# Two-layer hybrid decoder trunk: gate and up products with the stream stationary and the weights moving, the activations transposed afterwards

## The chip, the cores and the metric

The kernel runs on one core of one Trainium2 chip. Its time is the device time of one launch in microseconds; of three runs before the change the median is 1235.31 us (1235.24 to 1237.77). A profile of one execution stands beside it, whose span, from the first to the last instruction, is 1231.7 us. Engines are named as in the profile: PE is TensorE's matmul row and PEld its row of weight loads, DVE is VectorE, ACT is ScalarE, POOL is GpSimd, and SP issues most of the transfers.

## The reference

256 tokens of 1024 features pass through two layers. Each layer is a half-step feed-forward network, a mixing block (three branches, gated and projected), and a second half-step feed-forward network; a last RMSNorm ends it. Everything is float32.

```python
D_MODEL = 1024; SEQ = 256; DEPTH = 2; D_FF = 2816

def swiglu(x, w_gate, w_up, w_down):
    return (jax.nn.silu(x @ w_gate) * (x @ w_up)) @ w_down

for l in range(DEPTH):
    h = h + 0.5 * swiglu(rmsnorm(h, ffn1_norm[l]), ffn1_w_gate[l], ffn1_w_up[l], ffn1_w_down[l])
    u = rmsnorm(h, mix_norm[l])
    ...                                        # latent attention, differential attention, pooling
    h = h + merged @ w_out[l]
    h = h + 0.5 * swiglu(rmsnorm(h, ffn2_norm[l]), ffn2_w_gate[l], ffn2_w_up[l], ffn2_w_down[l])
return rmsnorm(h, final_norm)
```

The change touches `x @ w_gate` and `x @ w_up` of the four feed-forward networks: 1024 features in, 2816 out, for 256 tokens.

## The kernel before, in words

Every large product is made of three matmuls (`mm3`, lines 162 to 165). Each operand is held as a high part of 12 bits and a low part, both float32r; the product is high by high, low by high and high by low, added up in one PSUM bank. The stream's parts (`uhi`, `ulo`, eight tiles of 128 features by 256 tokens) come from `Norm`; they carry the norm's gain, but not yet each token's factor `r`. A weight tile is 1 MB: one transfer on SP's queue (line 150), then `wsplit` makes the parts in two pieces of 1024 columns each, the high one by a cast on ACT (line 158) and the low one by a subtraction on DVE (line 159). There are three buffers each for the raw tile, the high and the low part, so a cast may start when the matmuls are done with the tile three before it.

In a matmul one operand is stationary (128 by 128, loaded by a weight load) and the other moves through. The two kinds of product in this kernel are:

- Weights stationary: out comes transposed (features on the partitions, 256 tokens along the free dimension), and each matmul moves 256 columns, the tokens. The gate and up products are of this kind, and so are a few in the mixing block.
- Stream stationary (`gemm_tokens`, line 167): the tokens are on the partitions, 128 at a time, and each matmul moves 512 columns of weights. The down products, the gates and most of the mixing block are of this kind.

A feed-forward network (`ffn`, line 265) goes over the 2816 columns in eleven chunks of 256. A chunk takes one tile of gate weights and one of up weights, 48 matmuls for each (2 output tiles of 128 columns, 8 feature tiles, 3 products). In the first chunk of a network the halves of the stream are done one after the other, since its second half is only just being made. The token factors are needed along the free dimension here; `Norm.row` (line 238) spreads them with one small matmul (line 244). The products are multiplied by the factors on DVE (lines 302 and 304), the gate goes through Silu on ACT (line 307), DVE multiplies gate and up (line 309), and `split_evac` splits the result into `ghi` (ACT, line 258) and `glo` (DVE, line 259). These are already in the layout that the down product wants as its stationary operand.

The program is written in order, and a scheduler of the language places the instructions in each engine's queue before the launch; on the chip each queue then runs strictly in its order, with semaphores between the engines. PSUM has four banks for products (`acc`), three for transposes and scores (`tr`) and one for attention outputs.

Of the kernel before, what the change touches and what calls it, by code (L numbers as in the profile page):

```python
# [44 lines left out]
def plan():  # L45
    """Weight tiles in the order of their use: (array, layer, first row tile, row tiles, first column, columns)."""
# [5 lines left out]
    def ffn(layer, pre):  # L52
        for c in range(0, DFF, S):
            for w in ("gate", "up"):
                add(f"{pre}_w_{w}", layer, 0, KD, c, S)
        for half in range(2):
            for k in range(0, KF, 4):
                add(f"{pre}_w_down", layer, k, min(4, KF - k), half * 512, 512)
# [27 lines left out]
def trunk(ctx, tc, x, xt, positions, wall, small, lamrow, fnorm, out):  # L86
# [51 lines left out]
    # the input's loads, which go between those of the first weights  # L138
# [28 lines left out]
    def gemm_tokens(specs, xh, xl, n, before=None, tail=1):  # L167
        """Products with tokens on the partitions: one bank for each half of the tokens.

        The first half of the tokens is done ahead of the second in the last tiles, tail of them."""  # L170
# [3 lines left out]
        for part in parts:  # L174
            w = [(s[2] + j, hi[:, j, :], lo[:, j, :]) for s in part for hi, lo in (wsplit(s),) for j in range(s[3])]
            if before and part is parts[-1]:
                before()
            order = [(k, wh, wl, t) for k, wh, wl in w for t in range(2)]
# [7 lines left out]
    def rsqrt_mean(dst, src, n):  # L186
        """dst = (src / n + eps) ** -0.5"""
# [3 lines left out]
    class Norm:  # L191
        """The transposed, scaled stream in two parts, and each token's factor, half by half."""
# [26 lines left out]
        def first(self, k):  # L219
            """A tile of the same from the input, which comes in both layouts."""  # L220
# [17 lines left out]
        def row(self):  # L238
            """The factors along the free dimension, on every partition."""
# [15 lines left out]
    def split_evac(hi, lo, src, scale=None):  # L255
        """PSUM or SBUF -> the two parts, times a constant or a column."""
# [8 lines left out]
    def ffn(l, pre, u, following, midway=None):  # L265
        ghi = [big([P, 8, S], F32R, "ghi") for _ in range(3)]
        glo = [big2([P, 8, S], F32R, "glo") for _ in range(3)]
        for c in range(0, DFF, S):
            if c == 1024 and midway:
                midway(g[:, 0, :2])  # L270
            # transposed products, weights stationary: two tiles of each
            opened = bool(opening)
            w = [wsplit((f"{pre}_w_{n}", l, 0, KD, c, S)) for n in ("gate", "up")]
            if c == 0:
                # a bank for each tile, so that the first half of the stream serves them all
                ps = [[b()[:, :S] for _ in range(2)] for b in (acc, trp)]
                halves = [range(0, 4), range(4, 8)]
                order = [(n, i, k) for ks in halves for n in range(2) for i in range(2) for k in ks]
                if opened:
                    order = [(n, i, k) for n in range(2) for k in range(KD) for i in range(2)]  # L280
            else:
                banks = [acc() for _ in range(2)]
                ps = [[b[:, i * S:(i + 1) * S] for i in range(2)] for b in banks]
                order = [(n, i, k) for n in range(2) for i in range(2) for k in range(KD)]
# [4 lines left out]
            if c == 0:  # L289
# [4 lines left out]
                rb = u.row()  # L294
            g = tp.tile([P, 2, S], F32, tag="A", name="g", bufs=4)
            sg = tp.tile([P, 2, S], F32, tag="B", name="sg")
# [553 lines left out]
```

## Time and profile before

| | |
|---|---|
| median of three runs | 1235.31 us |
| span of the profiled execution | 1231.7 us |
| median less that span | 3.6 us |
| PE busy | 1216.1 us, 99% of the span |
| PEld busy | 1108.6 us, 90% |
| DVE busy | 792.4 us, 64% |
| ACT busy | 576.9 us, 47% |
| mean granted clock of TensorE | 0.999 |
| read from memory | 210.85 MB, 172 GB/s over the span |

The profile gives no launch time of its own for that execution; what lies around its span is taken as the difference to the median. Busy time is the union of an engine's instructions. Matmuls overlap in their pipeline: the mean duration of one is longer than the distance between the starts of two, so the cost of a stream of them is read from the starts in the timeline, not from the mean durations. In a timeline row the columns are start, duration, engine, line, operation, tiles and shapes, and the count of merged instructions.

### The profile page before, as it was taken

Reading aid. Unit: us, or ns where it says so; the run is one execution under the profiler, and the core shown is the slowest. Engines: PE = TensorE matmul, PEld = TensorE weight load, DVE = VectorE, ACT = ScalarE, POOL = GpSimd, SP = SyncE. Lnnn points to the kernel's source line nnn. Section 1 sums busy time; section 2 is a strip of 40 time slices with the busy share of each in tenths; the row PEclk is TensorE's granted clock in tenths of the full one; section 3 lists DMA queues with packets and bytes.
Section 4 is the critical chain, followed back from the end, with each engine's and each line's share of the span. In section 5 each row is a group of like instructions: output and inputs, shape, how many; then the busy total and the mean of one; then the engine's idle time right before and its main releaser. Section 6 shows DMA issues by size and latency. Waiting matters only on the chain.

```text
span 1231.7 us, 19142 instructions
## 1 busy us (share of the span) xinstructions
PE 1216.1 (99%) x7912; PEld 1108.6 (90%) x7912; DVE 792.4 (64%) x1281; ACT 576.9 (47%) x891; POOL 69.3 (6%) x126
## 2 busy tenths in 40 slices
PE   7999999999999999999999999999999999999997
PEld 7999989998788899998899998899978888999986
DVE  6776655777757666664576664568686485766653
ACT  5454444446544554443454443455455444544442
POOL 0000000700100000000000000024010000000000
PEclk9999999999999999999999999999999999999999
DMA  8655455325345545554555555544343554455551
GB/s 276 239 184 181 175 181 191 120 93 189 137 171 176 192 172 179 181 191 168 187 199 176 191 182 188 175 146 145 110 165 135 177 202 171 171 188 188 189 171 68
DMA packets 34631, 213.13 MB, mean 173 GB/s; under 512 B 4080, under 2 KB 5488, under 8 KB 10992
## 3 DMA queue, kind: packets, MB, share of 16 engines
q1 hardware_dynamic: 33408, 210.52, 48.3%
q10 hardware_dynamic: 1136, 1.40, 0.4%
q8 instruction: 62, 1.02, 0.3%
q14 instruction: 25, 0.20, 0.1%
HBM read 210.85 MB, written 1.05 MB: 172 GB/s over the span
## 4 chain that ended last, share of the span: by engine, by line
PE 94%; DVE 3%; issue 2%; ACT 0%; DMA 0%; SPq 0%; POOLq 0%; POOL 0%
PE acc L163 28%; PE acc L164 28%; PE acc L165 28%; PE o L589 2%; PE tr L555 2%; PE tr L582 1%; PE tr L546 1%; PE tr L206 1%; DVE lo L159 1%; PE tr L163 1%; PE tr L165 1%; PE tr L164 1%; DMA xT<-xt 0%; PE tr L602 0%; PE acc L658 0%
## 5 line engine op out<-in xcount | busy, mean ns | idle before, releaser
L158 ACT CAST hi<-raw 128x1024 fp32r<-128x1024 f32 (+2 forms) x416 | 403.6, 1005 | 512.4 <-issue 326.3
L159 DVE TENSOR_TENSOR lo<-raw,hi 128x1024 fp32r<-128x1024 f32 (+2 forms) x416 | 481.4, 1173 | 223.1 <-ACT hi L158 222.2
L163 PE MATMUL acc<-uhi,hi 128*128 128x256 f32 x1536 | 439.2, 286 | 5.6 <-ACT hi L158 5.6
L165 PE MATMUL acc<-uhi,lo 128*128 128x256 f32 x1536 | 437.7, 285 | 1.5 <-DVE lo L159 1.5
L164 PE MATMUL acc<-ulo,hi 128*128 128x256 f32 x1536 | 437.7, 285 | 0.0
L163 PEld LDWEIGHTS acc<-uhi,hi 128*128 128x128 f32 x1536 | 296.7, 193 | 5.8 <-ACT hi L158 5.6
L165 PEld LDWEIGHTS acc<-uhi,lo 128*128 128x128 f32 x1536 | 296.6, 193 | 2.3 <-DVE lo L159 2.1
L164 PEld LDWEIGHTS acc<-ulo,hi 128*128 128x128 f32 x1536 | 296.8, 193 | 0.3
L164 PE MATMUL acc<-lo,ghi 128*128 128x512 f32 x352 | 137.4, 390 | 0.0
L165 PE MATMUL acc<-hi,glo 128*128 128x512 f32 x352 | 137.3, 390 | 0.0
L163 PE MATMUL acc<-hi,ghi 128*128 128x512 f32 x352 | 137.2, 390 | 0.0
L164 PE MATMUL acc<-lo,uhi 128*128 128x512 f32 (+1 forms) x256 | 99.6, 389 | 0.0
L163 PE MATMUL acc<-hi,uhi 128*128 128x512 f32 (+1 forms) x256 | 99.4, 390 | 0.0
L165 PE MATMUL acc<-hi,ulo 128*128 128x512 f32 (+1 forms) x256 | 98.8, 386 | 0.0
L163 PEld LDWEIGHTS acc<-hi,ghi 128*128 128x128 f32 x352 | 66.1, 188 | 13.5
L165 PEld LDWEIGHTS acc<-hi,glo 128*128 128x128 f32 x352 | 66.1, 188 | 13.5
L164 PEld LDWEIGHTS acc<-lo,ghi 128*128 128x128 f32 x352 | 66.1, 188 | 13.5
L304 DVE TENSOR_TENSOR g<-acc,rb 128x512 f32<-128x512 f32 x40 | 27.7, 693 | 78.5 <-PE acc L165 78.5
L574 ACT ACTIVATE e<-e,mx 128x128 f32<-128x128 f32 (+1 forms) x96 | 42.8, 446 | 57.4 <-DVE mx L570 35.4
L304 DVE TENSOR_TENSOR sg<-acc,rb 128x512 f32<-128x512 f32 x40 | 27.7, 692 | 49.6 <-PE acc L165 49.6
L164 PEld LDWEIGHTS acc<-lo,uhi 128*128 128x128 f32 x256 | 48.1, 188 | 9.7 <-issue 1.3
L163 PEld LDWEIGHTS acc<-hi,uhi 128*128 128x128 f32 x256 | 48.0, 188 | 9.3 <-issue 0.7
(199 smaller groups left out, 1222.4 us busy)
## 6 DMA issues: line engine op xcount, KB each, us to landing
raw<-wall SPq DMA_DIRECT2D x184, 1024.0 KB, 4.8
raw<-wall SPq DMA_DIRECT2D x10, 512.0 KB, 3.5
raw<-wall SPq DMA_DIRECT2D x18, 256.0 KB, 5.4
raw<-wall SPq DMA_DIRECT2D x4, 832.0 KB, 4.4
raw<-wall SPq DMA_DIRECT2D x2, 768.0 KB, 4.1
xT<-xt SPq DMA_DIRECT2D x8, 128.0 KB, 4.6
h<-x SPq DMA_DIRECT2D x4, 256.0 KB, 5.8
fn<-fnorm ACTq DMA_DIRECT2D x1, 512.0 KB, 3.8
```

Source lines behind the costliest of these rows:

```text
L158: nc.scalar.copy(out=hif[:, ks], in_=rawf[:, ks])
L159: nc.vector.tensor_tensor(out=lof[:, ks], in0=rawf[:, ks], in1=hif[:, ks].bitcast(F32), op=ALU.subtract)
L163: nc.tensor.matmul(ps, lhsT=lh, rhs=rh, start=start, stop=False)
L164: nc.tensor.matmul(ps, lhsT=lh, rhs=rl, start=False, stop=False)
L165: nc.tensor.matmul(ps, lhsT=ll, rhs=rh, start=False, stop=stop)
L206: nc.tensor.transpose(out=ps[:, (i * 2 + t) * P:(i * 2 + t + 1) * P], in_=h[:, t, k * P:(k + 1) * P], identity=ident)
L304: nc.vector.tensor_tensor(out=dst, in0=banks[n].rearrange("p (i s) -> p i s", i=2), in1=rbb, op=ALU.mult)
L546: nc.tensor.matmul(ps[:, i * nk:(i + 1) * nk], lhsT=qT[:, hd, qt * P:(qt + 1) * P], rhs=kT[:, hd, :nk], start=True, stop=True)
L555: nc.tensor.matmul(ps[:, i * nk:(i + 1) * nk], lhsT=dqT[a:a + 32, hd // 2, qt * P:(qt + 1) * P], rhs=dkT[a:a + 32, hd // 2, :nk], start=Tr ...
L574: nc.scalar.activation(out=e[:, sl], in_=e[:, sl], func=AF.Exp, bias=mx[:, i:i + 1], scale=-(2.0 ** -(hd + 1)) if slope else -1.0, accum_o ...
L582: nc.tensor.transpose(out=ptr[:, j * P:(j + 1) * P], in_=e[:, j * P:(j + 1) * P], identity=ident)
L589: nc.tensor.matmul(o[:, hd * 64:(hd + 1) * 64], lhsT=eT[:, j * P:(j + 1) * P], rhs=v[:, kt, hd * 64:(hd + 1) * 64], start=(kt == 0), stop= ...
```

## The change

The two products are turned round. The stream's parts become the stationary operand and the weights move, 512 columns at a time, as in `gemm_tokens`. The host packs gate and up columns of a network in alternating blocks of 512 (`ffn1_gu`, `ffn2_gu`; 5632 columns), and the kernel goes over them in five chunks of 512 plus one of 256, whose gate and up columns share a tile. A weight tile is again 1 MB, 4 feature tiles by 512 columns, and there are 22 in a network as before. The outputs now have tokens on the partitions, so `r` is a scalar of each partition: Silu on ACT reads the gate bank with `scale=r`, and one DVE instruction multiplies the up bank by `r` and by the gate. The result `g` has to be transposed for the down product: `turned` does it with 128 by 128 transposes on PE, two feature tiles by two token halves in one `tr` bank, and splits the bank into `ghi` and `glo`. The transposes of a chunk are issued in the next chunk, between its gate and its up product; those of the last chunk at the start of the down product. `Norm.row` is no longer called in `ffn`.

```diff
     def ffn(layer, pre):
-        for c in range(0, DFF, S):
-            for w in ("gate", "up"):
-                add(f"{pre}_w_{w}", layer, 0, KD, c, S)
+        for c in range(0, 2 * DFF, 1024):
+            blocks = range(c, min(c + 1024, 2 * DFF), 512)
+            order = [(b, k) for k in (0, 4) for b in blocks] if c == 0 else [(b, k) for b in blocks for k in (0, 4)]
+            for b, k in order:
+                add(f"{pre}_gu", layer, k, 4, b, 512)
...
-    def gemm_tokens(specs, xh, xl, n, before=None, tail=1):
+    def gemm_tokens(specs, xh, xl, n, before=None, tail=1, early=None):
...
             if before and part is parts[-1]:
                 before()
+            if early and part is parts[0]:
+                early()
...
-        for c in range(0, DFF, S):
+        def turned(c, g):
+            for j in range(0, g[0].shape[1] // P, 2):
+                ptr = trp()
+                for i in range(2):
+                    for t in range(2):
+                        nc.tensor.transpose(out=ptr[:, (i * 2 + t) * P:(i * 2 + t + 1) * P],
+                                            in_=g[t][:, (j + i) * P:(j + i + 1) * P], identity=ident)
+                k = c // P + j
+                split_evac(ghi[k // 8][:, k % 8:k % 8 + 2, :].rearrange("p k s -> p (k s)"),
+                           glo[k // 8][:, k % 8:k % 8 + 2, :].rearrange("p k s -> p (k s)"), ptr)
+        pending = None
+        for c in range(0, DFF, 512):
+            n = min(512, DFF - c)
             if c == 1024 and midway:
-                midway(g[:, 0, :2])
-            w = [wsplit((f"{pre}_w_{n}", l, 0, KD, c, S)) for n in ("gate", "up")]
-            ...
-            for n, i, k in order:
-                wh, wl = w[n]
-                ms = slice(i * P, (i + 1) * P)
-                mm3(ps[n][i], wh[:, k, ms], wl[:, k, ms], u.xh(k), u.xl(k), k == 0, k == KD - 1)
+                midway(g[0][:, :2])
+            spec = lambda b, k: (f"{pre}_gu", l, k, 4, b, 512)
             if c == 0:
+                ps = [[b() for _ in range(2)] for b in (acc, trp)]
+                for k0 in (0, 4):
+                    for m in range(2):
+                        wh, wl = wsplit(spec(m * 512, k0))
+                        for k in range(4):
+                            for t in range(2):
+                                tk = slice(t * P, (t + 1) * P)
+                                mm3(ps[m][t], u.xh(k0 + k)[:, tk], u.xl(k0 + k)[:, tk], wh[:, k, :], wl[:, k, :],
+                                    k0 + k == 0, k0 + k == KD - 1)
...
-                rb = u.row()
-            g = tp.tile([P, 2, S], F32, tag="A", name="g", bufs=4)
-            ...
-            times(sg, 0)
-            nc.scalar.activation(out=sg, in_=sg, func=AF.Silu)
-            times(g, 1)
-            nc.vector.tensor_tensor(out=g, in0=g, in1=sg, op=ALU.mult)
-            k = c // P
-            split_evac(ghi[k // 8][:, k % 8:k % 8 + 2, :], glo[k // 8][:, k % 8:k % 8 + 2, :], g)
+            elif n == 512:
+                ps = []
+                for m in range(2):
+                    ps.append(gemm_tokens([spec(2 * c + m * 512, k) for k in (0, 4)], u.xh, u.xl, 512))
+                    if m == 0:
+                        turned(*pending)
+            else:
+                both = gemm_tokens([spec(2 * c, k) for k in (0, 4)], u.xh, u.xl, 512, lambda: turned(*pending))
+                ps = [[b[:, m * n:(m + 1) * n] for b in both] for m in range(2)]
+            g = []
+            for t in range(2):
+                r = u.r[:, t:t + 1]
+                sg = tp.tile([P, n], F32, tag="B", name="sg")
+                nc.scalar.activation(out=sg, in_=ps[0][t], func=AF.Silu, scale=r)
+                gt = tp.tile([P, n], F32, tag="A", name="g", bufs=4)
+                nc.vector.scalar_tensor_tensor(out=gt, in0=ps[1][t], scalar=r, in1=sg, op0=ALU.mult, op1=ALU.mult)
+                g.append(gt)
+            pending = c, g
...
-                             tail=1 if nxt else 2)
+                             tail=1 if nxt else 2, early=(lambda: turned(*pending)) if half == 0 else None)
```

Outside the four networks' gate and up parts the queues of all five engines hold the same instructions in the same order as before; SP's and POOL's are the same throughout. Two places where they differ matter for what follows. In the rows the first name behind the arrow is the operand that moves, the second the stationary one; the numbers tell one tile from another. The first place is PE's queue in the first network. Before, the first chunk's end and the second chunk's start, with the small matmul of `Norm.row`:

```order
L163 MATMUL tr_170<-uhi_100,hi_149 128x256
L164 MATMUL tr_170<-ulo_101,hi_149 128x256
L165 MATMUL tr_170<-uhi_100,lo_150 128x256
L244 MATMUL tr_282<-dg_279,ones_98 128x256
L163 MATMUL acc_326<-uhi_100,hi_297 128x256
L164 MATMUL acc_326<-ulo_101,hi_297 128x256
L165 MATMUL acc_326<-uhi_100,lo_298 128x256
```

Now, in the second chunk, the end of its gate product, the eight transposes of the first chunk's `g`, and the start of its up product:

```order
L167 MATMUL acc_318<-hi_352,ulo_101 128x512
L280 MATMUL tr_383<-ident_80,g_311 128x128
L280 MATMUL tr_383<-ident_80,g_315 128x128
L280 MATMUL tr_383<-ident_80,g_311 128x128
L280 MATMUL tr_383<-ident_80,g_315 128x128
L280 MATMUL tr_390<-ident_80,g_311 128x128
L280 MATMUL tr_390<-ident_80,g_315 128x128
L280 MATMUL tr_390<-ident_80,g_311 128x128
L280 MATMUL tr_390<-ident_80,g_315 128x128
L165 MATMUL acc_397<-hi_400,uhi_100 128x512
L166 MATMUL acc_397<-lo_401,uhi_100 128x512
```

The row of line 244 is gone, the matmuls are 512 wide, and eight transposes stand between gate and up. The second place is ACT's queue in one chunk of the second network. Before, in the course of one chunk of 256 (casts of weight tiles, Silu, split of `g`):

```order
L158 CAST hi_4498<-raw_4497 128x1024 x2
L258 CAST ghi_4110<-g_4367 128x512
L158 CAST hi_4506<-raw_4505 128x1024
L307 ACTIVATE sg_4490<-sg_4490 128x512
L158 CAST hi_4506<-raw_4505 128x1024
```

Now, in the course of one chunk of 512 (the casts of its four weight tiles, Silu of its own gate banks, the split of the transposed chunk before it, and the cast for the next chunk):

```order
L160 CAST hi_3915<-raw_3914 128x1024 x2
L160 CAST hi_3947<-raw_3946 128x1024 x2
L160 CAST hi_3995<-raw_3994 128x1024 x2
L160 CAST hi_4027<-raw_4026 128x1024 x2
L320 ACTIVATE sg_4058<-acc_3912,r_3746 128x512
L320 ACTIVATE sg_4062<-acc_3913,r_3746 128x512
L262 CAST ghi_3608<-tr_3978 128x512
L262 CAST ghi_3608<-tr_3985 128x512
L160 CAST hi_4069<-raw_4068 128x1024 x2
```

Four instructions that wait for PE now stand together ahead of the cast of the next chunk's first tile.

More of the change, by code (lines that the diff above doesn't have):

```diff
@@ L267, in ffn @@
         glo = [big2([P, 8, S], F32R, "glo") for _ in range(3)]
-        for c in range(0, DFF, S):
+        opened = bool(opening)
+        def turned(c, g):
[8 more added lines that the diff above has]
+                           glo[k // 8][:, k % 8:k % 8 + 2, :].rearrange("p k s -> p (k s)"), ptr)
@@ L269, in ffn @@
+        pending = None
+        for c in range(0, DFF, 512):
+            n = min(512, DFF - c)
             if c == 1024 and midway:
-                midway(g[:, 0, :2])
-            opened = bool(opening)
-            w = [wsplit((f"{pre}_w_{n}", l, 0, KD, c, S)) for n in ("gate", "up")]
+                midway(g[0][:, :2])
+            spec = lambda b, k: (f"{pre}_gu", l, k, 4, b, 512)
             if c == 0:
[L276 to L284, printed above, removed]
@@ L285, in ffn @@
-            for n, i, k in order:
-                wh, wl = w[n]
-                ms = slice(i * P, (i + 1) * P)
-                mm3(ps[n][i], wh[:, k, ms], wl[:, k, ms], u.xh(k), u.xl(k), k == 0, k == KD - 1)
-            if c == 0:
+                ps = [[b() for _ in range(2)] for b in (acc, trp)]
[7 more added lines that the diff above has]
+                                    k0 + k == 0, k0 + k == KD - 1)
@@ L293, in ffn @@
                 u.factor()
-                rb = u.row()
-            g = tp.tile([P, 2, S], F32, tag="A", name="g", bufs=4)
-            sg = tp.tile([P, 2, S], F32, tag="B", name="sg")
-            rbb = rb.rearrange("p (o s) -> p o s", o=1).broadcast_to([P, 2, S])
-            def times(dst, n):
-                if c == 0:
-                    for i in range(2):
-                        nc.vector.tensor_tensor(out=dst[:, i, :], in0=ps[n][i], in1=rb, op=ALU.mult)
-                else:
-                    nc.vector.tensor_tensor(out=dst, in0=banks[n].rearrange("p (i s) -> p i s", i=2), in1=rbb, op=ALU.mult)
-            times(sg, 0)
-            nc.scalar.activation(out=sg, in_=sg, func=AF.Silu)
-            times(g, 1)
-            nc.vector.tensor_tensor(out=g, in0=g, in1=sg, op=ALU.mult)
-            k = c // P
-            split_evac(ghi[k // 8][:, k % 8:k % 8 + 2, :], glo[k // 8][:, k % 8:k % 8 + 2, :], g)
+            elif n == 512:
[16 more added lines that the diff above has]
+            pending = c, g
         nxt = following() if following else None
@@ L793, in packed_weights @@
 def packed_weights(inputs):
-    arrays = {k: inputs[k] for k in ("ffn1_w_gate", "ffn1_w_up", "ffn1_w_down", "w_in", "mla_w_uq", "w_out",
-                                     "ffn2_w_gate", "ffn2_w_up", "ffn2_w_down")}
+    arrays = {k: inputs[k] for k in ("ffn1_w_down", "w_in", "mla_w_uq", "w_out", "ffn2_w_down")}
+    for pre in ("ffn1", "ffn2"):
+        w = [inputs[f"{pre}_w_{n}"] for n in ("gate", "up")]
+        arrays[f"{pre}_gu"] = np.concatenate([m[:, :, c:c + 512] for c in range(0, DFF, 512) for m in w], axis=2)
     ukv = inputs["mla_w_ukv"].reshape(DEPTH, P, NH, 2, 64)
```

## The prediction

> **What bounds the kernel now.** I read the page first: which engine is busy, and whose work makes the chain that ended last.
>
> ```profile
> PE 1216.1 (99%) x7912; PEld 1108.6 (90%) x7912; DVE 792.4 (64%) x1281; ACT 576.9 (47%) x891; POOL 69.3 (6%) x126
> ...
> PE 94%; DVE 3%; issue 2%; ACT 0%; DMA 0%; SPq 0%; POOLq 0%; POOL 0%
> ```
>
> PE is 94% of the chain and DVE's 3% lies in the mixing block and at the ends. A busy 99% alone does not say that PE never waits, since matmuls overlap. So the next view is PE's own waits (who was waited for, us in total, times, longest):
>
> ```profile
> PE acc L163 <- ACT hi L158: 5.6, 1, 5.6
> PE acc L165 <- DVE lo L159: 1.5, 2, 1.0
> ```
>
> The 5.6 us is the start of the program, before the first weights, and the 1.5 us are two pieces of the very first tile. After that PE is not held in a network. What a stage costs is then the sum of the distances between matmul starts, and the timeline gives them. First the gate and up product of the second network, from its first chunk's end to the down product:
>
> ```profile
> 441.78 0.28 PE L165 MATMUL tr<-uhi,lo 128*128 128x256 f32 x1
> 441.90 0.60 PE L244 MATMUL tr<-dg,ones 128*128 128x256 f32 x2
> 442.15 0.47 PE L163 MATMUL acc<-uhi,hi 128*128 128x256 f32 x1
> 442.45 0.28 PE L164 MATMUL acc<-ulo,hi 128*128 128x256 f32 x1
> ...
> 557.40 0.28 PE L165 MATMUL acc<-uhi,lo 128*128 128x256 f32 x1
> 557.52 0.40 PE L163 MATMUL acc<-hi,ghi 128*128 128x512 f32 x1
> ```
>
> Ten chunks with two tiles of 48 matmuls are 960 matmuls from 442.15 to 557.52, that is 115.37 us. The first of them took 0.30 to the next instead of 0.12, so 115.2 us are left: **0.120 us for a matmul of 256 columns**, without a gap. Then the down product, whose 512-wide form the change brings:
>
> ```profile
> 557.52 0.40 PE L163 MATMUL acc<-hi,ghi 128*128 128x512 f32 x1
> ...
> 587.69 0.39 PE L164 MATMUL acc<-lo,ghi 128*128 128x512 f32 x1
> 587.92 0.43 PE L206 MATMUL tr<-ident,h 128*128 128x128 f32 x2
> 588.11 0.48 PE L165 MATMUL acc<-hi,glo 128*128 128x512 f32 x1
> 588.43 0.40 PE L163 MATMUL acc<-hi,ghi 128*128 128x512 f32 x1
> ```
>
> 134 matmuls from 557.52 to 587.92 are 30.40 us: **0.2269 us for 512 columns**. Two of 256 cost 0.240. In both forms each matmul carries some 13 ns beyond a part that doubles with the columns (2 x 0.120 - 0.2269 = 0.0131).
>
> **The change part by part.** *The products.* A network has 22 tiles: 1056 matmuls of 256 become 528 of 512. Behind the first chunk 960 x 0.120 = 115.2 becomes 480 x 0.2269 = 108.9, 6.3 less; the first chunk's 96 x 0.120 = 11.5 becomes 48 x 0.2269 = 10.9, 0.6 less. Four networks make 27.7. The first network starts slowly, though:
>
> ```profile
> 15.48 0.42 PE L165 MATMUL acc<-uhi,lo 128*128 128x256 f32 x1
> 15.69 0.41 PE L163 MATMUL acc<-uhi,hi 128*128 128x256 f32 x1
> ...
> 17.05 0.28 PE L165 MATMUL acc<-uhi,lo 128*128 128x256 f32 x1
> 17.17 0.28 PE L163 MATMUL acc<-uhi,hi 128*128 128x256 f32 x1
> ```
>
> Until about 16.5 us the distance is 0.21, then 0.12. No 512-wide matmul runs at the slow pace in this trace; between twice 0.21 (no gain) and the usual gain I take half for that chunk, so 27.4 in all. The step's moment may shift, and half of a shift is what it costs; I bound it by 3.4 us, a third of the 10.9 us between the first matmul (5.6) and the step, so 1.7 us either way. The first tile's pieces arrive as before and each carries the same work; only the wait for the first low part now comes behind one matmul of 512 instead of three of 256, 0.2 us, which lies within that bound.
>
> *The transposes.* Five groups of eight and one of four in a network, 176 in all. The nearest row is the transposes of the mixing block, the same form between 512-wide matmuls, waiting for DVE as these do:
>
> ```profile
> 393.25 0.39 PE L165 MATMUL acc<-hi,y 128*128 128x512 f32 x1
> 393.48 1.03 PE L716 MATMUL tr<-ident,m 128*128 128x128 f32 x8
> 394.27 0.48 PE L163 MATMUL acc<-hi,y 128*128 128x512 f32 x1
> 394.58 0.39 PE L164 MATMUL acc<-lo,y 128*128 128x512 f32 x1
> ...
> 410.70 0.49 PE L716 MATMUL tr<-ident,m 128*128 128x128 f32 x3
> ```
>
> From 393.48 to 410.70 stand eight transposes and 72 matmuls: 17.22 - 72 x 0.2269 = 0.88. A group thus costs 0.88: 0.79 itself, the rest in the slower restart (0.31). Twenty groups are 17.6. The groups of four come as one and three; the two transposes at 587.92 took 0.19, and 0.32 - 0.23 = 0.09 at the restart, so I take 4 x 0.095 + 2 x 0.09 = 0.56, 2.2 for four networks. Together **19.8**. Below, without restarts, it is 176 x 0.095 = 16.7; above, if none overlapped, 176 times the 0.27 of a lone one, 47.5. Since the rows quoted are the same operation in the same surroundings, I stay with 19.8.
>
> *What goes away on PE:* line 244 in four networks, 442.15 - 441.90 = 0.25 and 0.18 at the restart, 0.43 each, 1.7.
>
> *ACT and DVE.* These rows (groups by line and shape: total busy and mean ns) price their work:
>
> ```profile
> L158 ACT CAST hi<-raw 128x1024 fp32r<-128x1024 f32 x368 | 372.5, 1047 | 448.4 <-issue 296.8 <-PE acc L165 104.4 <-PE acc L164 27.0
> L707 ACT ACTIVATE gate<-acc,rh 128x512 f32<-128x512 f32 x24 | 16.4, 683 | 18.9 <-PE acc L165 18.9
> L307 ACT ACT_TABLE_LOAD x4 | 5.1, 1283 | 2.1 <-DVE sg L302 2.1
> L159 DVE TENSOR_TENSOR lo<-raw,hi 128x1024 fp32r<-128x1024 f32 x368 | 445.4, 1225 | 177.6 <-ACT hi L158 176.7
> L309 DVE TENSOR_TENSOR g<-g,sg 128x512 f32<-128x512 f32 x44 | 30.4, 692 | 1.9 <-ACT sg L307 0.5
> L258 ACT CAST ghi<-g 128x512 fp32r<-128x512 f32 x44 | 27.0, 614 | 5.1 <-DVE g L309 5.1
> ```
>
> For 512 columns DVE had eight low parts and eight instructions of 0.69 (lines 304, 309, 259); now eight and four. It loses 2.8 of work and stays below 62% of the 22.7 us. ACT keeps its count. Neither is on the path, so this is worth nothing by itself, as long as the weights' parts come in time; that is the place where the change adds waits. In ACT's queue two Silu wait for the gate product, two splits wait for the transposes behind it, and behind these stands the cast of the next chunk's first tile. Counted from the gate's end: Silu 2 x 0.68, splits 2 x 0.61, a first piece of cast 1.05, its low part on DVE 1.23, together 4.9 us, say 5.3 with the signals. PE meanwhile has eight transposes and the up product's two tiles, 0.9 + 48 x 0.2269 = 11.8. The margin is 6.5 us: hidden. In a network's first chunk the gate ends one tile before the next chunk, 24 x 0.2269 = 5.4, and three of the four Silu there are preceded by a table load of 1.28; no splits yet: 1.28 + 1.37 + 1.05 + 1.23 = 4.9, nearly all of the margin. The last chunk's transposes wait for Silu and the multiplication of half a bank, with five matmuls (1.1 us) between; that may fall short by 0.3. I put 0.2 on each of these seven places, 1.4, between nothing and 0.5 each, 3.5.
>
> *Transfers.* SP's queue is unchanged; a tile is asked for every 24 x 0.2269 = 5.4 us instead of 5.8, as in the down product, where PE did not wait:
>
> ```profile
> raw<-wall SPq DMA_DIRECT2D x184, 1024.0 KB, 4.8
> ```
>
> A load of 4.8 starts when the low part three tiles earlier is done, two tiles ahead of need. Worth nothing. The scalar `r` and the packing cost nothing on the path either: they change operands, not counts.
>
> **The sum:** -27.4 + 19.8 - 1.7 + 1.4 = -7.9 us on the span of 1231.7, so 1223.8; with the 3.6 us between span and median, 1227.4. I say **1227.4 us**.
>
> [...]
>
> **The rivals.** *Stalls eat part of it.* If the close places cost more, or the chain behind the tables of the first network (DVE makes them between weight parts) holds PE once for some us, 2 to 5 us of the gain go: 1229.5 to 1232.8. For it: the margin of 0.5 us in the first chunk. Against: two tiles' margin elsewhere. *They eat all of it:* 8 us more of the same, 1233 to 1237.8, within 0.2% of before.
>
> *ACT's queue becomes the bound (slower).* If the nine instructions of a chunk on ACT slip far enough behind Silu, each next chunk starts late. It decides from a lateness of 6.5 us on; with 1 us in each of the 24 chunks it is 24 - 9.3 = +14.7, 1250. For it: four waiting instructions now stand ahead of a cast. Against: ACT was busy 47% and its work does not grow.
>
> *The gain of width isn't there (slower).* If the 13 ns belong to the kind of product (which operand is stationary) and not to each matmul, the products would save nothing: +19.8 - 1.7 + 1.4 = +19.5, 1254.8. [...] Against: 0.120/256 is 0.469 ns a column and 0.2269/512 is 0.443, in the two forms the change swaps, and the new form is that of the down product instruction by instruction.
>
> That the matmuls would not be 512 wide is excluded by the queue.
>
> **How the numbers follow.** The forecast has 0.78, part of it eaten 0.10, all of it 0.05, ACT's queue 0.05, no gain of width 0.02. A change of 0.2%, 2.5 us, is about what this measurement tells from none: below 1232.8 is faster. So faster is 0.78 + 0.10 = 0.88, the same 0.05, slower 0.07. The range starts at the lowest sum: no restarts in the transposes (16.7), no stall, and the clock's step 1 us earlier, -27.4 + 16.7 - 1.7 - 1.0 = -13.4, 1221.9. Of this corner I keep 1222.5. It ends at 1232.5, where the second case does. Beyond it lie 0.12 and the tail of the forecast.
>
> **What would show it.** In the changed profile: starts 0.227 apart in the gate and up products, 480 matmuls behind the first chunk and 44 transposes in about 114 us from the first chunk's end to the down product (before: 115.4 after the row of line 244); about 0.88 for each group of eight; PE's instructions down from 7912 to 5968; PE waits of no more than some 0.5 us in a network. Wrong would be distances of 0.24 or more between the matmuls, groups well over 1 us, or PE waiting for a high or low part behind a chunk's first tile.

## The result, and the profile of the changed kernel

The changed kernel takes **1225.25 us** (median of four executions, 1221.34 to 1225.94), the kernel before 1235.28 beside it (four, 1231.12 to 1237.77): a ratio of **0.992, 95% interval 0.9893 to 0.9947**. Forecast were 1227.4 us, in a range of 1222.5 to 1232.5. The profiled execution took 1224.84 us with a span of 1223.1.

The page of the changed kernel, the rows on busy time and on the chain that ended last:

```profile
PE 1207.8 (99%) x5968; PEld 1013.9 (83%) x5968; DVE 732.0 (60%) x1177; ACT 579.0 (47%) x894; POOL 67.7 (6%) x126
...
PE 95%; DVE 3%; issue 2%; ACT 0%; DMA 0%; SPq 0%; POOLq 0%; POOL 0%
```

PE has 1944 instructions less and is still the chain. Its own waits (who was waited for, us in total, times, longest):

```profile
PE acc L165 <- ACT hi L160: 5.5, 1, 5.5
PE acc L166 <- DVE lo L161: 1.2, 1, 1.2
PE acc L165 <- DVE k L540: 1.0, 2, 0.5
...
```

The first two are the opening. The third and the two rows behind it, of 0.5 each, lie in the mixing blocks: in no network does PE wait. The timeline of the second network, at its last full group of transposes (L280) and at the seam to the down product:

```profile
545.24 0.39 PE L167 MATMUL acc<-hi,ulo 128*128 128x512 f32 x1
545.48 1.03 PE L280 MATMUL tr<-ident,g 128*128 128x128 f32 x8
...
546.58 0.40 PE L166 MATMUL acc<-lo,uhi 128*128 128x512 f32 x1
...
551.58 0.40 PE L167 MATMUL acc<-hi,ulo 128*128 128x512 f32 x1
551.81 0.27 PE L280 MATMUL tr<-ident,g 128*128 128x128 f32 x1
551.84 0.47 PE L165 MATMUL acc<-hi,ghi 128*128 128x512 f32 x1
```

From 546.58 to 551.58 stand 22 matmuls: 5.00 / 22 = 0.227 each. The group of eight with its restart is 546.58 - 545.48 - 0.227 = 0.87.

To see where the 8.6 us of span went, the program is cut at the first transposes of the stream in each half (L206 before, L210 after). The columns of this view that matter here: from and to, length, busy time and instructions of PE; PEclk, near the end, is the granted clock. The kernel before:

```profile
0.00:199.91 199.91, 192.80 (x1330) 181.26 (x1331) 126.42 (x191) 95.67 (x128) 4.76 (x13) 1.00 0.59 205
199.91:429.30 229.39, 228.48 (x1290) 196.80 (x1290) 163.34 (x348) 116.66 (x225) 29.76 (x54) 1.00 0.43 155
429.30:587.92 158.62, 158.62 (x1201) 152.98 (x1200) 97.22 (x113) 70.31 (x86) 1.70 (x1) 1.00 0.51 182
618.80:776.99 158.19, 158.19 (x1199) 152.67 (x1198) 98.05 (x114) 69.50 (x87) 0.70 (x1) 1.00 0.51 183
807.53:1036.93 229.40, 228.36 (x1289) 196.79 (x1289) 163.18 (x348) 116.64 (x225) 29.60 (x54) 1.00 0.44 155
1036.93:1231.70 194.77, 188.26 (x1331) 177.39 (x1329) 113.05 (x134) 81.35 (x103) 2.81 (x3) 0.99 0.47 164
```

The changed kernel:

```profile
0.00:195.51 195.51, 188.81 (x845) 155.69 (x845) 112.38 (x165) 94.71 (x128) 3.27 (x13) 1.00 0.59 210
195.51:426.60 231.09, 230.06 (x1289) 197.90 (x1289) 163.13 (x348) 116.77 (x225) 29.63 (x54) 0.99 0.44 154
426.60:582.74 156.14, 156.14 (x716) 129.24 (x714) 81.89 (x87) 71.27 (x87) 1.71 (x1) 1.00 0.54 185
613.61:769.23 155.62, 155.62 (x713) 129.00 (x713) 82.90 (x88) 70.39 (x88) 0.70 (x1) 1.00 0.54 186
799.78:1030.86 231.08, 230.04 (x1289) 197.81 (x1289) 163.11 (x348) 116.79 (x225) 29.61 (x54) 0.99 0.43 153
1030.86:1223.10 192.24, 185.74 (x845) 153.68 (x843) 97.48 (x108) 82.28 (x104) 2.82 (x3) 1.00 0.47 167
```

| stage | before | after | difference |
|---|---|---|---|
| start and first network | 199.91 | 195.51 | -4.40 |
| mixing, first layer | 229.39 | 231.09 | **+1.70** |
| second network | 158.62 | 156.14 | -2.48 |
| third network | 158.19 | 155.62 | -2.57 |
| mixing, second layer | 229.40 | 231.08 | **+1.68** |
| fourth network and end | 194.77 | 192.24 | -2.53 |

(Between these stages lie the halves of the stream that stayed the same to 0.01.) Three networks gain 2.5 us each. Two things ask for an explanation: the first network gains 4.4, and the mixing blocks, in which PE does the same work in the same order, take 1.7 us more each.

The first is the step of the clock. At the start matmuls of 512 columns follow one another at 0.427 us, until this place in the opening of the changed kernel:

```profile
11.92 0.63 PE L167 MATMUL acc<-hi,ulo 128*128 128x512 f32 x1
12.35 0.63 PE L165 MATMUL acc<-hi,uhi 128*128 128x512 f32 x1
...
13.05 0.40 PE L167 MATMUL acc<-hi,ulo 128*128 128x512 f32 x1
13.29 0.39 PE L165 MATMUL acc<-hi,uhi 128*128 128x512 f32 x1
```

The record of the granted clock has the step at 12.87, that of before at 16.59. Half of 3.72 us is 1.86, and 2.48 and 1.86 are 4.34 of the 4.40.

The second is the clock again. The timeline of the first mixing block of the changed kernel, in its differential attention:

```profile
323.26 0.60 PE L595 MATMUL tr<-ident,e 128*128 128x128 f32 x4
323.79 1.12 PE L568 MATMUL tr<-d 32*128 32x256 f32 x4
324.84 1.10 PE L602 MATMUL o<-v,eT 128*128 128x64 f32 x8
325.88 1.13 PE L568 MATMUL tr<-d 32*128 32x256 f32 x4
326.94 0.79 PE L166 MATMUL acc<-lo,uhi 128*128 128x512 f32 x1
327.53 0.63 PE L167 MATMUL acc<-hi,ulo 128*128 128x512 f32 x1
327.95 0.63 PE L165 MATMUL acc<-hi,uhi 128*128 128x512 f32 x1
```

For 3.68 us PE has transposes, scores with 32 rows and outputs of 64 columns, without an idle moment that the profile shows. Behind them the large matmuls start 0.427 apart instead of 0.227, for the length of one window of 3.41 us (a halved window, from here on):

```profile
323.48:326.89 3.41, 3.41 (x20) 2.43 (x18) 2.51 (x6) 1.74 (x2) 0.00 (x0) 1.00 0.33 139
326.89:330.31 3.42, 3.42 (x9) 2.70 (x9) 2.22 (x9) 2.19 (x8) 0.00 (x0) 0.50 0.15 24
```

The same happens at 931.05. Half of 3.41 is 1.7: the loss of a mixing block. 326.89 lies 92.0 times 3.413 behind the step at 12.87, and 931.05 another 177.0 times: from the step on, the windows run through this trace in one grid. Counted back on it, the window that ends at the step, 9.45 to 12.87, is the first in which PE is busy throughout (3.42 us, and 2.22 in the window ahead of it); in the kernel before it is the one from 13.17 to 16.59 (3.42, and 2.91 ahead of it).

### The profile page after: what moved, and what is told of

Read it like the earlier page. It is cut to its first block, busy times and chain, and to the rows that moved or that the text cites. A ratio compares the mean times of both kernels' runs of the same rounds, so it can differ in the third digit from the quotient of the medians.

```text
span 1223.1 us, 15172 instructions
## 1 busy us (share of the span) xinstructions
PE 1207.8 (99%) x5968; PEld 1013.9 (83%) x5968; DVE 732.0 (60%) x1177; ACT 579.0 (47%) x894; POOL 67.7 (6%) x126
## 4 chain that ended last, share of the span: by engine, by line
PE 95%; DVE 3%; issue 2%; ACT 0%; DMA 0%; SPq 0%; POOLq 0%; POOL 0%
PE acc L165 27%; PE acc L166 27%; PE acc L167 27%; PE o L602 2%; PE tr L280 2%; PE tr L568 2%; PE tr L167 1%; PE tr L166 1%; PE tr L165 1%; PE tr L595 1%; PE tr L559 1%; PE tr L210 1%; DVE lo L161 1%; DMA xT<-xt 0%; PE tr L615 0%
## 5 line engine op out<-in xcount | busy, mean ns | idle before, releaser
L165 PE MATMUL acc<-hi,uhi 128*128 128x512 f32 (+1 forms) x896 | 352.9, 394 | 5.5 <-ACT hi L160 5.5
L166 PE MATMUL acc<-lo,uhi 128*128 128x512 f32 (+1 forms) x896 | 351.3, 392 | 1.2 <-DVE lo L161 1.2
L167 PE MATMUL acc<-hi,ulo 128*128 128x512 f32 (+1 forms) x896 | 350.2, 391 | 0.0
L165 PEld LDWEIGHTS acc<-hi,uhi 128*128 128x128 f32 x896 | 169.6, 189 | 39.5 <-ACT hi L160 5.5
L166 PEld LDWEIGHTS acc<-lo,uhi 128*128 128x128 f32 x896 | 169.8, 190 | 36.0 <-DVE lo L161 1.7
L167 PEld LDWEIGHTS acc<-hi,ulo 128*128 128x128 f32 x896 | 169.7, 189 | 34.0
L320 ACT ACTIVATE sg<-acc,r 128x512 f32<-128x512 f32 (+1 forms) x48 | 31.0, 653 | 55.8 <-PE acc L167 53.4
L165 PE MATMUL acc<-uhi,hi 128*128 128x256 f32 x192 | 55.6, 290 | 0.0
L166 PE MATMUL acc<-ulo,hi 128*128 128x256 f32 x192 | 55.2, 288 | 0.0
L167 PE MATMUL acc<-uhi,lo 128*128 128x256 f32 x192 | 55.0, 288 | 0.0
```

The lines of the kernel that those rows point to most:

```text
L165: nc.tensor.matmul(ps, lhsT=lh, rhs=rh, start=start, stop=False)
L166: nc.tensor.matmul(ps, lhsT=lh, rhs=rl, start=False, stop=False)
L167: nc.tensor.matmul(ps, lhsT=ll, rhs=rh, start=False, stop=stop)
L320: nc.scalar.activation(out=sg, in_=ps[0][t], func=AF.Silu, scale=r)
```

## The experiments

Times are medians of executions beside the kernel before on the same chip, and stages and spans those of the profiled execution. The experiments ran on four chips, one each for the first four, the next four, the next three and the last. The spans of the kernel before at a mean clock of 0.999 are 1228.8 to 1229.7 on all of them, and so spans are also compared between chips. Where "undisturbed" spans of single executions are compared, they are such with a mean clock of 0.999 or more: no trace with that mean has a halved window between the first step and the last few us, while of three traces with 0.998 two have one. The changed kernel's undisturbed span is 1219.4 to 1219.6.

**Halves again.** What belongs to a matmul, and what to the kind of product?

```diff
+    def mm3n(ps, lh, ll, rh, rl, start, stop):
+        for l_, r_, a, z in ((lh, rh, start, False), (lh, rl, False, False), (ll, rh, False, stop)):
+            step = 512 if a or z else 256
+            for i in range(0, 512, step):
+                nc.tensor.matmul(ps[:, i:i + step], lhsT=l_, rhs=r_[:, i:i + step], start=a, stop=z)
```

> The changed kernel with its gate and up products moved in halves of 256 columns again: same stationary stream, same tiles, transposes and order; of each accumulation only the first and the last matmul stay 512 wide. PE has 1936 matmuls more. Theory A (the 13 ns belong to each matmul, whatever is stationary): 1936 x 0.0131 = 25.4 us more than the changed kernel's 1225.3, so about 1250.7, starts 0.120 apart. Theory B (they belonged to the kind of product, not to the matmul): no difference, about 1225. [...]

Measured: 1248.94 us (1247.49 to 1250.22), ratio to before 1.0126 (1.0094 to 1.0158). The second network:

```profile
431.55:594.10 162.55, 162.55 (x1199) 154.70 (x1198) 81.95 (x87) 71.14 (x87) 1.70 (x1) 1.00 0.50 178
```

162.55 against 156.14: 6.41 us for 484 split matmuls in this network, **13.2 ns each**. The product with the stream stationary costs, in halves, what the old one did, and with the transposes on top the kernel is slower than before. Theory A holds.

**No transposes.** What do they cost in all?

```diff
-                ptr = trp()
-                for i in range(2):
-                    for t in range(2):
-                        nc.tensor.transpose(...)
+                src = g[j // 2][:, :S].rearrange("p (o s) -> p o s", o=1).broadcast_to([P, 2, S])
```

> The changed kernel without its 176 transposes on PE: the two parts of the activations are split from the untransposed products in SBUF, so the feed-forward results are not the reference's; ACT and DVE keep their instructions. Theory A (20 groups of 0.88 and 4 of 0.56, nothing hidden): 19.8 us less, about 1205.5. Theory B (the restart behind a group is not a cost of its own): 176 x 0.095 = 16.7 less, about 1208.5. Theory C (PE also loses time to the waits of the splits): more than 22 less, under 1203.

Measured: 1204.99 us (1202.03 to 1205.83). The second network:

```profile
421.56:572.64 151.08, 151.08 (x671) 124.86 (x670) 81.87 (x87) 72.12 (x87) 1.71 (x1) 1.00 0.56 191
```

5.06 us less than 156.14, 20.2 for four networks; by undisturbed spans 1200.2 against 1219.5, 19.3. Theory A: their whole price is on the path, and no wait of the splits hides behind it.

**Transposes twice.**

```diff
-                for i in range(2):
+                for i in (0, 1, 0, 1):
                     for t in range(2):
                         nc.tensor.transpose(...)
```

> The changed kernel with each transpose made twice into the same bank, 352 in place of 176, in the same 24 groups. Theory A (0.095 for each transpose in a row, a restart once for each group): 176 x 0.095 = 16.7 us more, about 1242. Theory B (a transpose's price is that of a lone one, 0.27): 47 more, 1272. Theory C (the splits behind the longer groups come late and PE waits): more than 20 more.

Measured: 1243.79 us (1240.17 to 1244.53), 18.5 above the changed kernel's median; undisturbed 1238.4, 18.9 above. The second network:

```profile
433.37:594.29 160.92, 160.92 (x760) 134.06 (x758) 81.62 (x87) 71.25 (x87) 1.70 (x1) 1.00 0.52 179
```

4.78 us more for 44 transposes, 0.109 each, which is also the distance of their starts. So the group of eight is 8 x 0.109: the split into 0.095 for each and a restart was not right, though the group's 0.88 was. Theory A's sum of 16.7 is 2 us short by this; theories B and C fall.

**More work in the long stretches.** Does a window full of small matmuls halve the clock?

```diff
             ps = trp()
+            if g >= 4:
+                nc.tensor.matmul(ps, lhsT=u.hi[:, 0, :P], rhs=u.hi[:, :2, :].rearrange("p k s -> p (k s)"),
+                                 start=True, stop=True)
```

> The changed kernel with eight more matmuls of 512 columns (two in each of the two long stretches of each mixing block that hold only transposes, scores of 32 rows and outputs of 64 columns, 3.68 us each). They write a bank that the scores overwrite. Theory A (the clock is halved for 3.41 us behind a window of 3.41 us that lies in such a stretch, and costs 1.7 us each time): no such step in any execution, so mean clock 0.998 or more in all of them and times close together, at the undisturbed 1219.6 of span and 1.7 around it plus 8 x 0.235 = 1.9: 1221 to 1225, by the moment of the opening's step. Theory B (the steps come from something else, as chance or temperature): steps stay, mean clocks of 0.994 to 0.996 in most executions, and the median is 1.9 above the changed kernel's, 1227.

Measured: 1226.16 us (1223.14 to 1226.45), six executions with mean clocks of 0.995, 0.995, 0.997, 0.998, 0.998 and 1.000. In the profile the first block has no halved window, the second still has one:

```profile
927.71:931.13 3.42, 3.42 (x18) 2.39 (x18) 1.62 (x6) 1.09 (x4) 0.00 (x0) 1.00 0.03 5
931.13:934.54 3.41, 3.41 (x8) 2.66 (x9) 2.56 (x10) 2.74 (x6) 0.00 (x0) 0.50 0.00 0
```

The prediction of no step failed; two matmuls in a stretch were too few. The window at 927.71 is filled to 0.85 with scores and outputs and to 0.15 with the added matmuls. That gave a sharper form of the theory: for every window of the grid, the share of scores with 32 rows and outputs of 64 columns. The seven halved windows in the mixing blocks of the first six traces have 0.83 to 0.91, all other windows 0.81 or less. (A matmul counts from its start to the next one's start.) Transposes do not count with the small ones: the window of the halves run at 945.22 has 0.15 of them and 0.81 of the small matmuls, 0.96 together, and the clock stayed.

**Scores in pairs.** The stretch is made shorter than a window.

```diff
-        def scores_diff(g, m):
+        def scores_diff(g):
             qt, hds, nk = groups[g]
-            ps = trp()
+            ps = trp(), trp()
             for i, hd in enumerate(hds):
-                a = ((hd % 2) * 2 + m) * 32
-                nc.tensor.matmul(ps[:, i * nk:(i + 1) * nk], ...
+                for m in range(2):
+                    a = ((hd % 2) * 2 + m) * 32
+                    nc.tensor.matmul(ps[m][:, i * nk:(i + 1) * nk], ...
```

> The changed kernel with the scores of the differential attention issued head by head, both halves of a head in turn into two banks, so that neighbours use different rows of the array; the same matmuls. Theory A (the clock is halved behind each free-running window of 3.41 us that is filled by more than 0.81 to 0.83 with scores of 32 rows and outputs of 64 columns; all seven steps and no other window of six traces fit that): if neighbours now overlap, the long stretches get shorter than such a window (0.53 + 1.06 + 1.05 of 3.68), no step comes in any execution, mean clocks of 0.998 or more, and the span stays within 1 us of the changed kernel's undisturbed 1219.6 or up to 10 us below it. If neighbours don't overlap, the stretches stay and so do the steps. Theory B (steps have another cause): clocks of 0.994 to 0.996 in most executions, whatever the length of the stretches.

Measured: **1218.87 us** (1217.81 to 1221.46), ratio to before 0.9882 (0.986 to 0.9905). Five of six executions have clocks of 0.998 or more and spans of 1216.0 to 1218.0; one has 0.995; where its clock was halved no trace shows. The stretch that took 3.68 us, in this kernel:

```profile
314.21 0.60 PE L596 MATMUL tr<-ident,e 128*128 128x128 f32 x4
314.74 0.70 PE L569 MATMUL tr<-d 32*128 32x256 f32 x4
315.60 1.10 PE L603 MATMUL o<-v,eT 128*128 128x64 f32 x8 [0.15 <-DVE eT L598]
316.63 0.70 PE L569 MATMUL tr<-d 32*128 32x256 f32 x4
317.26 0.50 PE L166 MATMUL acc<-lo,uhi 128*128 128x512 f32 x1
```

Four scores take 0.63 to the next instruction's start instead of 1.06; the stretch is 3.05 long. Neighbours now read different rows of their operands, but they also write different banks, and no run separates the two. No position of a window in this trace reaches more than 0.74. Theory A in five executions of six. The sixth it does not explain: a mean clock of 0.995 is some 12 us at half clock (2 x 0.005 x 1205), of which the traces show 1 to 4 at the end of the program.

**Matmuls ahead of the first weights.**

```diff
+    wt = tp.tile([P, 512], F32, tag="C", name="wt")
+    nc.vector.memset(wt, 1.0)
+    wr = tp.tile([P, 512], F32R, tag="B", name="wr")
+    nc.vector.tensor_copy(out=wr, in_=wt)
+    pw = po.tile([P, 512], F32, tag="o", name="pw")
+    for i in range(14):
+        nc.tensor.matmul(pw, lhsT=wr[:, :P], rhs=wr, start=True, stop=True)
```

> The changed kernel with 14 matmuls of 512 columns on constants ahead of the first real one, while PE waits for the first weights (0 to 5.5 us). Theory A (the clock's first step needs one free-running window of 3.41 us with PE busy): the step comes at 5 to 8.5 us in place of 12.9, the first chunk is then bound by the arrival of the weights' parts (last low part of the first two tiles about 18.4 in the trace of the changed kernel), and the time is 1.5 to 2 us less, about 1223.5. The steps of the mixing blocks stay, so the spread between executions stays. Theory B (the first step is set by something else, as the time since the start): no difference or up to 1 us more.

Measured: 1223.2 us (1219.67 to 1225.18). Its opening:

```profile
1.90 5.87 PE L130 MATMUL pw<-wr 128*128 128x512 f32 x14 [1.90 <-DVE wr L127]
7.61 0.62 PE L172 MATMUL acc<-hi,uhi 128*128 128x512 f32 x2
```

The clock steps at 7.10. The first transposes of the stream behind the first network start at 163.60 instead of 164.99 (165.41 in a second profile of the changed kernel): 1.4 to 1.8 us gained. The undisturbed spans of 1217.9 and 1218.8 are 0.7 to 1.6 below 1219.5. The steps of the mixing blocks stay: three of six executions have clocks of 0.995, and the profiled one a halved window at 928.70. Theory A.

**ACT's queue, longer.** Is its margin what was reckoned? In the second kernel the count is nine.

```diff
-                nc.scalar.activation(out=sg, in_=ps[0][t], func=AF.Silu, scale=r)
+                for _ in range(4):
+                    nc.scalar.activation(out=sg, in_=ps[0][t], func=AF.Silu, scale=r)
```

> The changed kernel with each Silu made four times into the same tile, so that ACT's queue holds six more instructions of 0.68 us, 4.1 us, between a gate product's end and the next cast. Theory A (a margin of 6.5 us in a chunk, 0.5 in a first chunk): nothing in the chunks behind the first, up to 3.6 us in each first chunk, so 0 to 14 us more than 1225, and PE waits named by hi or lo only near first chunks. Theory B (the queue is already the bound): 4.1 us in each of the 24 chunks, about 1323.

> The same with each Silu nine times: sixteen more instructions of 0.68 us, 10.9 us. Theory A (margin of 6.5 us): each later chunk's first tile comes 4.4 us late, 20 times, and a first chunk's 10.4, four times: up to 130 us more, about 1350 at most, less if casts ahead of Silu build up a lead. Theory B (ACT has slack far beyond it, as its share of 47% would let one think): under 10 us more.

Measured, one execution each: 1226.23 and 1237.37 us. With four Silu, PE waits 0.54 for a high and 0.52 for a low part, both at the first tile behind the very first chunk, and nowhere else in a network. With nine, PE's waits begin:

```profile
PE acc L165 <- ACT hi L160: 7.3, 4, 5.6
PE tr L280 <- DVE g L323: 6.9, 3, 5.6
PE acc L166 <- DVE lo L161: 2.2, 3, 1.2
```

Of the 6.9 one is 5.65 long, in the first network, for `g` itself, from 31.10 to 36.75; PE stood idle, and the clock was halved from 34.98 on for 6.83 us. That network takes 11 us more, the second 1.9, the third 1.1. Theory A's upper figure is far off, and B's is passed by little. But the scheduler had put casts between the added Silu, so that the queue's order was not the one the margin of 6.5 us was counted in. What the second kernel shows: 262.5 us of Silu in place of 31.0, some 58 more in each network, cost 1 to 2 us a network behind the first. The figure of 6.5 itself stays untested; the 0.4 us for signals in it were the author's estimate.

**Both kernels once more.**

> The changed kernel itself, beside the next two. Theory A (halved windows come by chance of the window's phase: by the matmuls of its trace, 34% of the phases put no window over 0.81, 11% one and 55% two): about a third of the executions with a mean clock of 0.998 or more and spans of 1219 to 1220, the others at 1221.5 to 1224.5; median 1225, all of them 9 to 10 us below executions of the kernel before with the same clock (1229.4 of span at 0.999 to 1.0). Theory B (the changed kernel is slowed by steps that the kernel before doesn't have): no execution at 1219 to 1220, or a share far under a third, while the kernel before has half of its executions at 0.999.

Measured: 1224.93 us (1221.22 to 1225.89), ratio 0.9917 (0.99 to 0.9934). One of six executions has 0.999 and a span of 1219.4, one 0.998 and 1220.9, four 0.995 to 0.997 and 1223.0 to 1224.1. With the four of the result, two of ten are undisturbed, where theory A has a third; the shares agree with it as far as ten executions can tell.

> The kernel before itself, for a second profile. Theory A: a network behind the first takes 158.6 us from its first transposes of the stream to the next network's, as in the first profile, whatever the clock does elsewhere; the span is 1229.4 with no halved window in the mixing blocks and the first step at 13 us or earlier, 1231.7 with the first step at 16.6, and 3.4 us more with one halved window in each block. Theory B (the networks themselves vary between executions): 158.6 does not return within 0.2 us.

Measured: 1235.37 us (1232.58 to 1238.12, eight executions). Rows of its profile:

```profile
426.66:585.27 158.61, 158.61 (x1201) 152.97 (x1200) 97.20 (x113) 70.31 (x86) 1.70 (x1) 1.00 0.52 182
```

158.61 again, to 0.01. The clock stepped at 11.90 here, not 16.59, and the first network ended 2.6 us earlier; in the second mixing block this execution has a halved window, behind a share of 0.84. So neither belongs to the change: the kernel before has both, by the moment at which it meets the grid. Against itself this kernel measured 1.0016 (1.0002 to 1.0031); an interval from such steps is a little too sure.

Over all 59 executions of the kernel before with a recorded clock, 17 have 0.999 (spans 1228.8 to 1229.7, median 1229.5), six 0.997 (1230.85), one 0.996, 24 have 0.994 (1233.6) and eleven 0.993 (1236.3). None of the last 35 has a profile. A mean clock of 0.994 is some 14.6 us at half clock (2 x 0.006 x 1217), of which the traces show 1 to 4 at the end: three halved windows or more, where the two profiles of this kernel show none and one.

An estimate shows that the theory allows this. Take the distances of the matmul starts in its first profile from 190 to 1060 us, lengthened in a halved window as the large matmuls are there (0.227 to 0.427). Then move the grid through all its positions, with a halved window behind each one that is filled by more than 0.81. In 31% of the positions there is no halved window, in 12% one or two, in 57% three or four, since a halved window shifts the work behind it against the grid. It makes no difference whether the small ones are lengthened too. Of the 59 executions 29% have 0.999, 12% have 0.996 or 0.997, and 59% have 0.993 or 0.994.

**Both edits, on both kernels.**

> Both edits at once on the changed kernel: scores in pairs and the 14 matmuls on constants ahead of the first weights. Theory A (the two are independent): 6.4 and 1.2 us below the changed kernel, so spans of 1214.8 to 1216.5 and a median of 1217.7, with mean clocks of 0.998 or more in nearly all executions. Theory B (the gain of the pairs was the chance of phases on that chip): median 1222 to 1225 with clocks of 0.995 in half of the executions.

Measured: **1217.67 us** (1217.38 to 1218.15), ratio to before **0.9867** (0.9852 to 0.9882); all clocks 0.998 or 0.999. The forecast of 1217.7 for two independent edits is met, and the four executions lie within 0.8 us. This version beats both kernels.

> The kernel before with the same two edits as the combined run (scores in pairs, 14 matmuls on constants at the start), so that the change stands alone between two kernels without halved windows in the mixing blocks. Theory A (the change is worth four times the 2.48 us that the networks behind the first show, and nothing else): 9.9 us above the combined kernel's 1217.7, so 1227.6, with mean clocks of 0.998 or more. Theory B (part of the measured 10 us was the clock's doing): the distance is under 8 or over 12, 1225 or less or 1230 and more.

Measured: 1229.15 us (1228.02 to 1229.45), clocks 0.998 and 0.999, 11.5 above the other kernel, which ran on another chip. The stages of this kernel:

```profile
0.00:198.31 198.31, 195.11 (x1344) 181.95 (x1344) 127.22 (x193) 95.30 (x128) 5.00 (x13) 1.00 0.60 207
198.31:426.48 228.17, 226.77 (x1289) 194.70 (x1289) 163.23 (x348) 116.44 (x225) 29.60 (x54) 1.00 0.44 155
426.48:585.10 158.62, 158.62 (x1202) 152.98 (x1200) 97.36 (x113) 70.33 (x86) 1.70 (x1) 1.00 0.52 182
```

And of the changed kernel with the same edits:

```profile
0.00:194.25 194.25, 192.09 (x858) 158.09 (x859) 112.98 (x167) 95.02 (x128) 3.49 (x13) 1.00 0.59 211
194.25:422.35 228.10, 226.68 (x1289) 194.62 (x1289) 163.26 (x348) 116.42 (x225) 29.59 (x54) 1.00 0.45 155
422.35:578.49 156.14, 156.14 (x716) 129.29 (x714) 81.92 (x87) 71.36 (x87) 0.69 (x1) 1.00 0.53 185
```

Without halved windows the first mixing blocks agree to 0.07, and the networks behind the first differ by the same 2.48. Neither theory has 11.5: the 9.9 of theory A was short by 1.6, and this lies in the opening: the first stage differs by 4.06, though the clock steps at 7.04 and 7.59. At full clock PE in the kernel before loses time there, by the distances of the starts 0.87 us at 23.7 and 0.48 at 20.0, and its waits name low parts (0.9) and the factors' tile (0.3); in the changed kernel PE loses nothing between 12 us and the first transposes of activations. Why its parts come in time was not followed further.

## Why the prediction was right, and where not

| step of the prediction | forecast | measured |
|---|---|---|
| products, behind the first network | -6.9 a network | -7.0 (528 x 13.2 ns, from the halves) |
| groups of eight | 0.88 | 0.877, all twenty |
| groups of four, as one and three | 0.56 | 0.113 + 0.374 = 0.49 |
| transposes in all | +19.8 | +19.5 by the trace's groups; 19.3 to 20.2 without them |
| line 244 | -0.43 a network | the row is gone; not tried alone |
| one network without stalls | -2.38 (from -6.9, +4.95, -0.43) | -2.48, -2.57, -2.53 |
| stalls at seven close places | +1.4 | 0 |
| ACT, DVE, transfers | hidden | hidden |
| the clock's first step | up to 1.7 either way | 1.86 earlier |
| mixing blocks | 0 | +3.38, halved windows |
| span | 1223.8 | 1223.1 |
| from span to time | 3.6 | 1.74 |

**The forecast's main steps hold, each by its own run.** The 13 ns that each matmul carries beyond its columns go with the number of matmuls (the halves bring them back), and the transposes' price taken from the mixing block is that of the networks too, to 0.01 us a group. What the prediction said would show it stands in the trace: starts 0.227 apart, 113.33 us from the 49th matmul of the second network to its down product (about 114 were forecast), 5968 instructions, no wait in a network.

**Three steps failed, and partly took each other's place.** First, "*I put 0.2 on each of these seven places, 1.4*": there is no stall at any of them. Second, "*The step's moment may shift ... I bound it by 3.4 us*" (a third of 10.9 is 3.6): it shifted by 3.72 between the two profiles, and the second profile of the kernel before shows it another 1 us earlier than the changed kernel's. It is chance, not the change, and the term should not have been centred on one profile. Third, the prediction has no term for the clock inside the program; two halved windows took 3.38 us back. With 0 for stalls, -1.9 for the step and +3.4 for the windows, -7.9 becomes -7.9 - 1.4 - 1.9 + 3.4 = -7.8. The errors of these terms cancel almost wholly, so that the span came out within 0.7 us is partly luck. Of the 0.8 to -8.6 the transposes are 0.3 and the 2112 matmuls fewer, at 13.2 ns in place of 13.1, 0.2; 0.3, as much as was taken off for the cold first chunk, stays open.

**The largest error in the forecast time is a term of no engine:** "*with the 3.6 us between span and median, 1227.4*". Every execution here that has both figures has 1.7 to 1.9 us around its span. The profiled execution of before was simply not a median one: 1231.7 and 1.8 are 1233.5, between the levels of 1231.3 and 1235.4 at which most of its executions lie. 1.86 of the 2.56 us by which 1227.4 missed 1224.84 come from there.

**The rivals.** That the gain of width is not there fell with the halves: 13.2 ns for each matmul more. That ACT's queue becomes the bound fell: the profile has no such wait, and the kernel with four times the Silu loses 1 us (one execution). Stalls that eat a part: none. What in fact ate a part, in some executions, was not among the rivals, and it eats as much in the kernel before.

**What the change is worth.** Undisturbed spans of 1229.5 and 1219.5 give 10.0 us, which is four times 2.5. The medians of 1235.3 and 1225.3 give 10.0 as well, since in both kernels most executions have clocks that speak for halved windows. With both edits on both kernels it is 11.5, 1.6 of it in the opening.

## What to carry to other kernels

Count matmuls, not only columns: where each carries a fixed part (here 13 ns beside 107 for 256 columns), the wider moving side paid, as long as what turns the result back costs less (here 4.9 us against 7.0 a network), and that price could be read from the same operation elsewhere in the trace (0.88 for a group of eight, 0.877 measured). Before a span is compared with a median, look at how the executions of the kernel spread and at the granted clock of each: here a difference of 0.7% in a stage whose instructions did not change was the clock's. A stretch of 3.68 us with small matmuls cost 1.7 us beyond its own time where these filled a window of 3.41 us to 0.817 or more; shortening it to 3.05, here by the order of the scores, brought the ratio to before from 0.992 to 0.9882.

## What the runs showed of the hardware

In the mixing blocks the clock of TensorE was halved **without any idle time of PE** that a trace shows. In all fourteen traces, a window of 3.41 us of the grid was followed there by a halved one where scores with 32 rows and outputs of 64 columns filled 0.817 to 0.91 of it, 13 windows, and nowhere else; the fullest of the others has 0.805. No kernel was made to find the limit between these two shares, and which of the two kinds of matmul brings the halving about, and why, stays open. With PE idle the clock was halved too: from 34.98 on, within the 5.65 us of waiting (31.10 to 36.75) of the kernel with nine Silu, and at the end of the program, in the changed kernel behind a window without a matmul (1217.77 to 1221.18), in the kernel before behind one with 0.28 us of PE (1224.91 to 1228.32). A halved window cost 1.7 us in each mixing block (1.70 and 1.68), and a first step 3.72 us earlier went with 1.9 us less in the first stage (4.40 less 2.48). With both taken out, nearly all of the spread between executions is gone: four executions of the changed kernel lie within 0.8 us and six of the kernel before within 1.4, where seventeen of the unedited kernel before, beside the four, spread over 4.6.
